# Low parts of some weight blocks made by an accumulating transfer instead of VectorE

## The chip, the cores and the metric

The kernel runs on one core of a Trainium2 chip. The engines that matter here are TensorE (PE in the profile; its weight loads are PEld), VectorE (DVE), ScalarE (ACT), GpSimd (POOL) and SyncE (SP), whose queue issues nearly all transfers. Each engine works through its own list of instructions in a fixed order and waits on semaphores for the others. The metric is device time in microseconds (us) of one launch. Before the change the median of three runs was 957.13 us, from 956.89 to 957.25.

## The reference

The reference is a trunk of two layers on 256 tokens of width 1024. Each layer adds half a SwiGLU feed-forward block, an attention mixer with an input and an output projection, and half a second SwiGLU block:

```python
def swiglu(h, w_gate, w_up, w_down):
    return (jax.nn.silu(h @ w_gate) * (h @ w_up)) @ w_down
for i in range(DEPTH):                       # DEPTH = 2, D_MODEL = 1024, D_FF = 2816
    h = rmsnorm(x, ffn1_norm[i])
    x = x + 0.5 * swiglu(h, ffn1_w_gate[i], ffn1_w_up[i], ffn1_w_down[i])
    ...                                      # mixer: w_in, attention, memory attention, w_out
    h = rmsnorm(x, ffn2_norm[i])
    x = x + 0.5 * swiglu(h, ffn2_w_gate[i], ffn2_w_up[i], ffn2_w_down[i])
```

All data is float32. The four feed-forward blocks hold most of the work.

## The kernel before, in words

**Three products for one.** TensorE multiplies in fp32r, a shorter float32. To keep float32 accuracy every operand is split: `hi` is the operand rounded to fp32r, and `lo` is what is left, `raw - hi`. A product is then three matmuls, hi by hi, lo by hi and hi by lo. They are lines 508, 511 and 514 in `dense`; the second one, line 511, is the first that reads `lo` of the weights. A matmul has 128 rows of weights by 512 columns.

**Weights come in chunks of 1 MB.** A chunk of a gate/up stage holds 4 row blocks of 128 rows, with 256 gate columns and 256 up columns each, so 128 partitions by 2048 elements. Group `g` (0 to 10) is 256 of the 2816 columns, and `c` (0 or 1) is the half of the 1024 rows. A plain gate/up chunk feeds 24 matmuls. `loader` gives each chunk one of three `raw` buffers and issues its two loads from SP (line 291). `split_hi` makes `hi` on ScalarE in two casts of 128x1024 (line 335), and `split_lo` makes `lo` on VectorE in two subtractions of 128x1024 (line 353). Four pairs of `hi` and `lo` buffers go round: the fifth chunk can't be cast before TensorE is done with the first. A `raw` buffer is free for another load when its chunk's `lo` is made.

**Stages.** A feed-forward block is a gate/up stage and a down stage. In the last three of the four blocks, groups 3 and 4 of the gate/up stage are made by seven block products instead of eight (`pair_items`, named m1 to m7, with sums of raw blocks, `wsum`, as operands). Their chunks and products lie between the plain chunks. The order there is, after groups 0 to 2: m1, (5,0), m5, (5,1), m7, (6,0), m6, (6,1), m3, (7,0), (7,1), m2, (8,0), m4, (8,1), (9,0), (9,1), (10,0), (10,1). A product `m` has 12 matmuls, and its result tile is `pair_m`; a plain chunk's result is `gu`.

**The planner.** The order of all instructions is written out at build time by `Flow`: each engine has a time when it is free, every step books a duration, and the generators `loader`, `split_hi` and `split_lo` go on when their conditions hold on that clock. On the chip only the order and the semaphores are left.

**Round trips.** The product of gate and up is transposed through DRAM: `hd<-hb` and `hr<-hd` (lines 640 and 646) are in the same SP queue as the weight loads. GpSimd has small work here: the powers of -1/2 of the norms (line 529).

## Time and profile before

| | |
|---|---|
| median of 3 runs | 957.13 us |
| profiled execution, its own time | 956.95 us |
| its span (first to last instruction) | 955.2 us |
| mean granted TensorE clock | 1.000 |
| gate/up stages that the change touches | about 318 to 435, 494 to 612, 776 to 894 us |

A profiled execution gives, for each engine, every instruction with its start and duration. The span is 1.75 us shorter than the execution's own time, which has the launch around it. Windows are given in us from the span's start. In the timeline a row has start, duration, engine, line, operation, output and inputs, and in square brackets idle time and what ended it. The share of busy time of TensorE is near to full everywhere, since its matmuls overlap (one is shown with 0.39 us, and starts 0.227 us after the one before it); the waits and the starts tell more than the share.

### The profile page before, as it was taken

The page shows a single profiled execution, that of the slowest core. Times are in us where ns is not written, and L with a number is a line of the kernel's source. Part 1 is how long each engine was busy: PE and PEld are TensorE (multiplying, and loading weights), DVE is VectorE, ACT ScalarE, POOL GpSimd, SP SyncE. Part 2 cuts the span into 40 slices and gives each one's busy share as a digit, 9 for nine tenths or more (in the row PEclk, how much of TensorE's full clock was granted, in tenths as well). Part 3 has the DMA queues.
Part 4 walks back from the last instruction along what each step waited for, and adds up shares of the span by engine and source line. Part 5 has one row for each costly group of instructions (what it writes and reads, how often), then busy time and mean ns, then how long its engine had stood idle before and what let it go on. Part 6 is the DMA issues. An engine that isn't in the chain of part 4 may idle for free.

```text
span 955.2 us, 13249 instructions
## 1 busy us (share of the span) xinstructions
PE 946.8 (99%) x4489; PEld 777.3 (81%) x4489; DVE 796.1 (83%) x1437; ACT 578.6 (61%) x1102; POOL 110.7 (12%) x160
## 2 busy tenths in 40 slices
PE   8999999999999999999999999999999999999998
PEld 7888888888877888888888888888887778888886
DVE  6767767688787899989889899896999888998884
ACT  6655555677676756647646656563676865665650
POOL 1000088322110100000000000000434200000000
PEclk9999999999999999999999999999999999999999
DMA  9988878486525376787746769775641367589751
GB/s 287 326 260 284 260 249 262 154 272 212 177 90 163 102 248 226 242 301 232 240 144 219 231 204 298 247 254 170 208 152 56 122 212 228 180 267 286 238 196 44
DMA packets 169294, 204.03 MB, mean 214 GB/s; under 512 B 9673, under 2 KB 144394, under 8 KB 169226
## 3 DMA queue, kind: packets, MB, share of 16 engines
q1 hardware_dynamic: 169226, 203.18, 66.3%
q8 instruction: 35, 0.57, 0.3%
q14 instruction: 33, 0.27, 0.1%
HBM read 188.99 MB, written 14.16 MB: 213 GB/s over the span
## 4 chain that ended last, share of the span: by engine, by line
PE 93%; DVE 4%; ACT 1%; DMA 1%; issue 0%; SPq 0%
PE gu L514 14%; PE gu L508 14%; PE gu L511 14%; PE acc L508 9%; PE acc L514 9%; PE acc L511 9%; PE pj L514 3%; PE pj L511 3%; PE pj L508 3%; PE pair_m L514 2%; PE pair_m L511 2%; PE pair_m L508 2%; DVE lo L353 1%; PE S L1335 1%; PE xtp L522 1%; PE AV L1416 1%
## 5 line engine op out<-in xcount | busy, mean ns | idle before, releaser
L335 ACT CAST hi<-raw 128x512 fp32r<-128x512 f32 (+1 forms) x469 | 339.1, 771 | 194.3 <-PE gu L514 75.5
L353 DVE TENSOR_TENSOR lo<-raw,hi 128x512 fp32r<-128x512 f32 (+1 forms) x469 | 394.6, 877 | 67.7 <-ACT hi L335 66.7
L514 PE MATMUL gu<-hi,xl 128*128 128x512 f32 x608 | 236.9, 390 | 0.4 <-DVE xl L559 0.4
L511 PE MATMUL gu<-lo,xh 128*128 128x512 f32 x608 | 236.8, 389 | 0.0
L508 PE MATMUL gu<-hi,xh 128*128 128x512 f32 x608 | 236.8, 389 | 0.0
L514 PEld LDWEIGHTS gu<-hi,xl 128*128 128x128 f32 x608 | 114.1, 188 | 24.5 <-DVE xl L559 0.8
L508 PEld LDWEIGHTS gu<-hi,xh 128*128 128x128 f32 x608 | 114.2, 188 | 23.5
L511 PEld LDWEIGHTS gu<-lo,xh 128*128 128x128 f32 x608 | 114.1, 188 | 23.5
L514 PE MATMUL acc<-hi,ht 128*128 128x512 f32 x280 | 109.5, 391 | 0.0
L508 PE MATMUL acc<-hi,ht 128*128 128x512 f32 x280 | 109.3, 390 | 0.0
L511 PE MATMUL acc<-lo,ht 128*128 128x512 f32 x280 | 109.1, 390 | 0.0
L511 PE MATMUL pj<-lo,xh 128*128 128x512 f32 x160 | 63.9, 400 | 0.0
L514 PE MATMUL pj<-hi,xl 128*128 128x512 f32 x160 | 63.8, 399 | 0.0
L508 PE MATMUL pj<-hi,xh 128*128 128x512 f32 x160 | 63.8, 399 | 0.0
L529 POOL TENSOR_TENSOR xr<-v,nhalf 128x1 f32<-128x1 f32 x12 | 11.7, 974 | 445.0 <-DVE v L527 445.0
L511 PEld LDWEIGHTS acc<-lo,ht 128*128 128x128 f32 x280 | 52.6, 188 | 10.9
L514 PEld LDWEIGHTS acc<-hi,ht 128*128 128x128 f32 x280 | 52.6, 188 | 10.8
L508 PEld LDWEIGHTS acc<-hi,ht 128*128 128x128 f32 x280 | 52.6, 188 | 10.7
L335 ACT CAST hi<-wsum 128x512 fp32r<-128x512 f32 x66 | 38.9, 620 | 20.5 <-DVE wsum L347 20.4
L623 ACT ACTIVATE sil<-gu,xr 128x256 f32<-128x256 f32 x76 | 35.7, 470 | 25.0 <-PE gu L514 24.9
L353 DVE TENSOR_TENSOR lo<-wsum,hi 128x512 fp32r<-128x512 f32 x66 | 42.5, 678 | 0.0
L529 POOL TENSOR_TENSOR hf<-v,nhalf 128x8 f32<-128x8 f32 (+1 forms) x20 | 31.7, 1584 | 90.1 <-DVE v L527 81.8
(231 smaller groups left out, 1356.6 us busy)
## 6 DMA issues: line engine op xcount, KB each, us to landing
raw<-in_ffn_w_down_dram SPq DMA_DIRECT2D x176, 256.0 KB, 4.3
raw<-in_ffn_w_gate_dram SPq DMA_DIRECT2D x86, 512.0 KB, 4.2
raw<-in_ffn_w_up_dram SPq DMA_DIRECT2D x86, 512.0 KB, 5.4
raw<-in_w_in_dram SPq DMA_DIRECT2D x32, 512.0 KB, 5.4
hd<-hb SPq DMA_DIRECT2D x44, 256.0 KB, 4.5
hr<-hd SPq DMA_DIRECT2D x44, 256.0 KB, 4.4
raw<-in_w_out_dram SPq DMA_DIRECT2D x8, 1024.0 KB, 4.8
raw<-in_w_mem_kv_dram SPq DMA_DIRECT2D x4, 1024.0 KB, 5.5
```

The source lines that it names most:

```text
L335: nc.scalar.copy(out=it.part(0, q, w), in_=src())
L353: nc.vector.tensor_sub(it.part(1, q, w), src(), it.part(0, q, w).bitcast(F32))
L508: nc.tensor.matmul(out=ps, lhsT=xh, rhs=wh, start=start, stop=False)
L511: nc.tensor.matmul(out=ps, lhsT=xh, rhs=wl, start=False, stop=False)
L514: nc.tensor.matmul(out=ps, lhsT=xl, rhs=wh, start=False, stop=stop)
L522: nc.tensor.transpose(out=dst, in_=src, identity=flip if flipped else ident)
L529: nc.gpsimd.tensor_tensor(out=dst, in0=v[:, :n], in1=nhalf[:, :n], op=ALU.pow)
L623: nc.scalar.activation(sil, ps[tb][:, 0:256], AF.Silu, scale=xt.r[tb])
L1335: nc.tensor.matmul(out=ss[e][:, pr, :nk], lhsT=q[rows, pr, :], rhs=k[rows, pr, :], start=i == 0, stop=i == len(passes) - 1)
L1416: nc.tensor.matmul(out=av[64 * e:64 * e + 64, pr, :], lhsT=vsrc(kb, pr, e), rhs=pts[e][:, pr, kb, :], start=(kb == 0), stop=(kb == nb - 1))
```

## The change

For four chunks in each of the last three gate/up stages, (6,1), (7,1), (8,1) and (9,1), VectorE's two subtractions are left out. ScalarE, after each cast to `hi`, writes minus that high part into the `lo` buffer: it rounds the raw block again with a factor of -1. Then GpSimd issues one transfer of 128x2048 that adds the raw block to what stands in `lo`. The planner books 7.0 us for it, and gives the `raw` buffer back after that. The lines after the new ones are moved down: line 335 is now 336, the new ScalarE step is line 339, the transfer is line 349, line 353 is now 371, lines 508 to 514 are 529 to 535, and the load of line 291 is 292.

```diff
@@ Item.__init__
             self.n, self.frees, self.takes, self.gives, self.guest = 1, 1, 0, 0, False
+            self.by_dma = False
@@ split_hi
                 nc.scalar.copy(out=it.part(0, q, w), in_=src())
                 t = flow.act(512 * w)
+                if it.by_dma:
+                    nc.scalar.activation(it.part(1, q, w), src(), AF.Copy, scale=-1.0)
+                    t = flow.act(512 * w)
                 it.hit[q:q + w] = [t] * w
+            if it.by_dma:
+                flow.spawn(lo_by_dma(it))
+
+    def lo_by_dma(it):
+
+        t = it.hit[3]
+        yield t
+        nc.gpsimd.dma_start(out=it.lo[0], in_=it.raws[0].raw, accum_op=ALU.add)
+        t = flow.now + 7.0
+        it.lot[0:4] = [t] * 4
+        yield t
+        raw_left[0] += it.frees
 
     def split_lo():
         for i, it in enumerate(items):
+            if it.by_dma:
+                continue
@@ plan
+    FOUR = ((6, 1), (7, 1), (8, 1), (9, 1))
+    BY_DMA = {(0, 1): (), (0, 2): FOUR, (1, 1): FOUR, (1, 2): FOUR}
@@ plan_ffn
                 gu[w] = add_chunk(parts(*w), 8, 2)
+                gu[w].by_dma = w in BY_DMA[l, nm]
```

The first place is ScalarE's list around chunk (6,1) of the first touched stage. Names carry the number of the chunk in the planner's list: 63 is the operand of m6, 64 is (6,1), 65 the operand of m3, 66 is (7,0) and 67 is (7,1). Before:

```order
L335 CAST hi63_0_3715<-wsum_3537 128x512
L335 CAST hi64_0_3778<-raw63_3701 128x1024 x2
L335 CAST hi65_0_3793<-raw61_3594 128x1024 x2
L335 CAST hi66_0_3827<-raw64_3728 128x1024 x2
L335 CAST hi67_0_3851<-raw65_3814 128x1024 x2
L623 ACTIVATE sil_3880<-gu0_3785,xr_2977 128x256
L655 CAST ht_3897<-hr_3841 128x512
```

And with the change:

```order
L336 CAST hi63_0_3715<-wsum_3537 128x512
L336 CAST hi64_0_3778<-raw63_3701 128x1024
L339 ACTIVATE lo64_0_3779<-raw63_3701 128x1024
L336 CAST hi64_0_3778<-raw63_3701 128x1024
L339 ACTIVATE lo64_0_3779<-raw63_3701 128x1024
L336 CAST hi65_0_3804<-raw61_3594 128x1024 x2
L336 CAST hi66_0_3824<-raw64_3728 128x1024 x2
L336 CAST hi67_0_3856<-raw65_3838 128x1024
L339 ACTIVATE lo67_0_3857<-raw65_3838 128x1024
L336 CAST hi67_0_3856<-raw65_3838 128x1024
L339 ACTIVATE lo67_0_3857<-raw65_3838 128x1024
```

Chunks 64 and 67 now take four steps of ScalarE each, with nothing else between them; the `sil` step has gone behind chunk 67.

The second place is SP's queue a little later, with what each row waits for: a DVE mark is VectorE's semaphore, a DMAHW mark one of the transfers that SP issues, and a DMASW mark one of the new transfers. `raw65` is loaded for chunk 67, `raw66` for the block of m2, `raw67` for (8,0) and `raw68` for (8,1). Before:

```order
L291 DMA raw65_3814<-in_ffn2_w_gate_dram 128x4x256 [waits DMAHW6_49,DMAHW5_49,DVE_49]
L291 DMA raw65_3814<-in_ffn2_w_up_dram 128x4x256
L291 DMA raw66_3834<-in_ffn2_w_gate_dram 128x4x256 [waits DVE_49]
L291 DMA raw66_3834<-in_ffn2_w_up_dram 128x4x256
L646 DMA hr_3841<-hd_3796 128x4x128 [waits DMAHW7_49,DMAHW2_49,Pool_49]
L291 DMA raw67_3856<-in_ffn2_w_gate_dram 128x4x256 [waits DMAHW1_49,DMAHW0_49,DVE_49]
L291 DMA raw67_3856<-in_ffn2_w_up_dram 128x4x256
L291 DMA raw68_3908<-in_ffn2_w_gate_dram 128x4x256 [waits DMAHW3_49,DMAHW4_49,DVE_49,Activation_49]
```

And with the change:

```order
L667 DMA hr_3834<-hd_3794 128x4x128 [waits DMAHW2_49,Pool_49]
L292 DMA raw65_3838<-in_ffn2_w_gate_dram 128x4x256 [waits DVE_49]
L292 DMA raw65_3838<-in_ffn2_w_up_dram 128x4x256 [waits DMAHW5_49]
L292 DMA raw66_3861<-in_ffn2_w_gate_dram 128x4x256 [waits DMAHW6_49,DMASW0_49]
L292 DMA raw66_3861<-in_ffn2_w_up_dram 128x4x256 [waits DMAHW7_49]
L292 DMA raw67_3864<-in_ffn2_w_gate_dram 128x4x256 [waits DMAHW1_49,DMAHW0_49,DVE_49]
L292 DMA raw67_3864<-in_ffn2_w_up_dram 128x4x256
L661 DMA hd_3949<-hb_3898 128x512 [waits DVE_49]
L292 DMA raw68_3956<-in_ffn2_w_gate_dram 128x4x256 [waits DMAHW4_49,DMAHW3_49,DMAHW5_49,DMASW1_49,Activation_49]
```

`raw65` now waits for VectorE's low part of chunk 65 instead of 64, `raw66` waits for the transfer of chunk 64, and `raw68` waits for the transfer of chunk 67.

The third place is GpSimd's list in the first two touched stages, where line 550 is the former line 529. With the change:

```order
L550 TENSOR_TENSOR xr<-v,nhalf 128x1 x2
L349 DMA lo_0_3779<-raw_3701 128x2048
L349 DMA lo_0_3857<-raw_3838 128x2048
L349 DMA lo_0_4026<-raw_3956 128x2048
L349 DMA lo_0_4105<-raw_4037 128x2048
L550 TENSOR_TENSOR xr<-v,nhalf 128x1 x2
L349 DMA lo_0_5389<-raw_5311 128x2048
L349 DMA lo_0_5467<-raw_5448 128x2048
L349 DMA lo_0_5636<-raw_5566 128x2048
L349 DMA lo_0_5715<-raw_5647 128x2048
L550 TENSOR_TENSOR xr<-v,nhalf 128x1
```

Before, the five `xr` steps stood there alone. The order of TensorE's instructions is the same before and after.

## The prediction

> **What bounds the kernel now.** I read first the engines' shares, then who TensorE waits for, then the three stages that the change touches. The page, the list of TensorE's waits over the whole span, and the busy time in the three gate/up stages and in a busy stretch of the first:

> ```profile
> PE 946.8 (99%) x4489; PEld 777.3 (81%) x4489; DVE 796.1 (83%) x1437; ACT 578.6 (61%) x1102; POOL 110.7 (12%) x160
> ...
> PE xtp L522 <- DMA x<-in_x_dram: 1.5, 2, 1.1
> PE warm L1621 <- POOL ident masks.py:199: 1.4, 1, 1.4
> PE otp L522 <- DVE of L1487: 0.5, 1, 0.5
> PE AV L1473 <- ACT PT L1349: 0.5, 1, 0.5
> PE gu L514 <- DVE xl L559: 0.4, 1, 0.4
> ...
> 318.00:435.00 117.00, 117.00 (x520) 96.92 (x519) 104.49 (x164) 69.95 (x109) 1.79 (x2) 1.00 0.72 233
> 494.00:612.00 118.00, 118.00 (x524) 97.77 (x523) 106.58 (x166) 70.43 (x108) 0.86 (x1) 1.00 0.75 241
> 776.00:894.00 118.00, 117.65 (x521) 97.11 (x520) 106.94 (x170) 72.39 (x113) 1.50 (x2) 1.00 0.74 234
> ...
> 400.00:410.00 10.00, 10.00 (x46) 8.26 (x44) 9.97 (x18) 5.91 (x8) 0.00 (x0) 1.00 1.02 323
> ```

> TensorE is the bound, and in the touched stages it is the whole bound: 520 matmuls in 117 us are 0.225 us each, the pace of its own stream, at a granted clock of 1.00. Of all its listed waits only 1.4 us lie behind 300 us, and none waits for a low part in these stages. VectorE is 89 to 91% busy there, ScalarE about 60%, the transfers 72 to 75% of the DMA engines, but all of that is done ahead of TensorE. So nothing that relieves VectorE can be seen at the end, and the question is only whether the new way of making `lo` is still done in time.

> How far ahead it is done is read at one chunk. The timeline around (6,1) of the first stage, ScalarE, VectorE and TensorE:

> ```profile
> 369.22 3.89 ACT L335 CAST hi<-raw 128x1024 fp32r<-128x1024 f32 x4
> 371.92 6.90 DVE L353 TENSOR_TENSOR lo<-raw,hi 128x1024 fp32r<-128x1024 f32 x6
> ...
> 378.04 0.39 PE L511 MATMUL gu<-lo,xh 128*128 128x512 f32 x1
> ```

> The first two casts of the row at 369.22 are this chunk's, the first two subtractions at 371.92 too (they end at about 374.3), and 378.04 is the first matmul on its `lo`, right after product m6. From the first cast to that matmul are 8.8 us, and the old way leaves 3.7 us over.

> **Part 1: VectorE loses, ScalarE gains.** The rows by form:

> ```profile
> L353 DVE TENSOR_TENSOR lo<-raw,hi 128x1024 fp32r<-128x1024 f32 x166 | 198.5, 1216 | 34.3 <-ACT hi L335 33.5 <-DMA grow<-in_mem_q_norm_dram 0.7
> L335 ACT CAST hi<-raw 128x1024 fp32r<-128x1024 f32 x166 | 168.8, 1049 | 106.0 <-PE gu L514 58.2 <-DMA raw<-in_ffn_w_up_dram 28.2 <-issue 10.6
> L571 ACT ACTIVATE junk<-x 128x512 bf16<-128x512 f32 x24 | 15.0, 624 | 0.0
> L335 ACT CAST hi<-raw 128x512 fp32r<-128x512 f32 x303 | 170.3, 619 | 88.3 <-PE acc L514 30.8 <-PE gu L514 17.4 <-issue 16.4
> ```

> 24 subtractions of 1.216 us, 29.2 us, leave VectorE. An ACTIVATE costs what a cast of the same width costs (624 and 619 ns), so 24 steps of 1.049 us, 25.2 us, come to ScalarE, 8.4 us a stage: from 60% to 67%. As work both count zero, since TensorE waits for neither; the cover is the lead of each chunk. But ScalarE's two extra steps lie in the chunk's own chain: four steps back to back took 3.89 us, with the hop to the next engine 4.0 us.

> **Part 2: the transfer.** 12 transfers of 1 MB that read two blocks and write one. No row shows an accumulating transfer, or one that GpSimd issues. The nearest rows are plain 1 MB transfers in one piece, issue to landing, and the spread of the loads between 360 and 410 us:

> ```profile
> raw<-in_w_out_dram SPq DMA_DIRECT2D x8, 1024.0 KB, 4.8
> raw<-in_w_mem_kv_dram SPq DMA_DIRECT2D x4, 1024.0 KB, 5.5
> ...
> DMA to landing us min/median/max: 4.1/5.2/9.6
> ```

> Call its time from issue to landing X. From below it is a plain transfer, 4.8. For the second read I add 1.05 MB at the 323 GB/s that the full engines moved (row at 400:410), 3.25 us: 8.1 to 8.8. From above it is the slowest landing, 9.6, plus a second read at the stage's mean of 234 GB/s, 4.5: 14.1. I take 8.5, by the 5.5 us row, since loads run beside it here. [...]

> Chunk (6,1): the low part is there at 369.22 + 4.0 + X = 373.2 + X, wanted at 378.04. It is late by X - 4.8: **3.7 us**. TensorE stands at this matmul, and all behind it moves by that.

> **Part 3: what is queued behind.** SP's queue and the timeline for (7,1) and (8,1):

> ```profile
> 374.30 0.37 SPq L291 DMA_DIRECT2D raw<-in_ffn_w_gate_dram  x1
> ...
> 379.97 1.05 ACT L335 CAST hi<-raw 128x1024 fp32r<-128x1024 f32 x1 [2.63 <-DMA raw<-in_ffn_w_up_dram]
> ...
> 385.52 0.37 SPq L291 DMA_DIRECT2D raw<-in_ffn_w_gate_dram  x1
> ...
> 391.64 0.39 PE L511 MATMUL gu<-lo,xh 128*128 128x512 f32 x1
> ...
> 396.62 0.39 PE L514 MATMUL gu<-hi,xl 128*128 128x512 f32 x1
> ...
> 398.58 0.47 ACT L623 ACTIVATE sil<-gu,xr 128x256 f32<-128x256 f32 x1
> 398.95 4.13 ACT L335 CAST hi<-raw 128x1024 fp32r<-128x1024 f32 x4
> ...
> 407.96 0.39 PE L511 MATMUL gu<-lo,xh 128*128 128x512 f32 x1
> ```

> (7,1): its load was issued at 374.30 and its cast began 5.67 us later. The load now waits for VectorE's part of the next chunk, which needs the casts after the four steps and ends at 373.2 + 1.0 + 2 x 1.2 = 376.6. Cast at 382.4, four steps, transfer: there at 386.4 + X. Wanted at 391.64 + (X - 4.8) = 386.8 + X. In time by 0.4, whatever X is: **0**.

> (8,1): its load waits for the transfer of (7,1), issue 386.4 + X, against 385.52 before. Cast at 392.1 + X; its buffers come free when (7,1) is done on TensorE, 397.0 + X - 4.8 = 392.2 + X, the same moment. Four steps and one `sil` of 0.5 between them, transfer: there at 396.7 + 2X, wanted at 407.96 + X - 4.8 = 403.2 + X. Late by X - 6.5: **2.0 us**.

> (9,1): its load doesn't wait for a transfer, and three chunks of TensorE time lie between its buffers' release and its use: 13.6 us, less 4.0 and 8.5. In time: **0**, as before.

> SP issues in order, so behind these waits also stand `raw66`, `raw67` and the round trips hd and hr; their results are wanted in the down stage, after 435, tens of us later: 0. On GpSimd nothing is queued behind the four issues until the next stage's `xr`.

> **The sum.** 5.7 us a stage. In the other two the distance from first cast to matmul is the same:

> ```profile
> 546.12 3.90 ACT L335 CAST hi<-raw 128x1024 fp32r<-128x1024 f32 x4
> 554.72 0.39 PE L511 MATMUL gu<-lo,xh 128*128 128x512 f32 x1
> ...
> 827.91 2.95 ACT L335 CAST hi<-raw 128x1024 fp32r<-128x1024 f32 x3
> 836.46 0.39 PE L511 MATMUL gu<-lo,xh 128*128 128x512 f32 x1
> ```

> 8.6 and 8.55 us against 8.82. Three stages are 17.1 us. On the profiled execution's 956.95 us that is 974.05; the median of the runs is 0.18 us above it, so I predict **974 us**. TensorE has no idle time behind the stages in which it could win this back. By X: 4.8 gives 957; 6.5 gives 962; 14.1 gives 9.3 + 7.6 = 16.9 a stage, 1008.

> **The rivals.**

> *Hidden.* X is near its lower bound, the transfers fit into the leads, and TensorE never waits. For it: the transfer needs no HBM, and the plain rows are at 4.8. Against it: two reads. Up to X = 5.4 it costs 3 x 0.6 = 1.8 us: 957 to 959. Chance 0.17. This is the case of no change, not slower.

> *Transfers far slower.* [...] At X = 20: 15.2 + 13.5 = 28.7 a stage, 86 us, 1043 us. No row speaks for or against it. Chance 0.13. [...]

> *Faster.* VectorE's relief shortens a wait of TensorE. There are 1.4 us of such waits after 300 us, and if all went it were 955.7 us, within 0.2%. Chance of more than that: 0.03.

> *ScalarE becomes the bound.* Its 67% is an average; if the `sil` steps that moved behind (7,1) held up the accumulators, each stage would lose about those 4 steps, 4.2 us, on top: 987 us. Against it: the accumulators of the next groups are others. Chance 0.05.

> **How the numbers follow.** The forecast, late at (6,1) and (8,1) with X from 5.4 to 14.1, has the remaining 0.62. The range takes in the hidden case and the upper bound of X: 957 to 1008. What this kernel's measurement can tell from no change is about 0.2%, 1.9 us. Faster 0.03, same 0.17, slower 0.80 (0.62 + 0.13 + 0.05).

> **What would show it.** In the profile of the changed kernel: the waits of TensorE get a row at the second matmul of a chunk (now line 532) that ends with the transfer, 12 or fewer times, with the longest near 3.7 us and a sum near 17. The transfers' time from issue to landing is X itself. ScalarE's new steps should take 1.05 us. The SP queue should wait about as long for the transfers as `raw68` is late. It is wrong if TensorE waits for none of this, if the transfers land within 5 us, or if (7,1) or (9,1) is a place of the largest wait.

## The result, and the profile after

The changed kernel takes 991.92 us, the median of 4 runs (990.29 to 994.95), beside 957.12 us for the kernel before on the same chip. The ratio is 1.036, with a 95% interval from 1.034 to 1.038: 34.8 us slower, where 17 were forecast. The profiled execution took 992.51 us, 35.6 more than the one of before.

The page of the changed kernel, TensorE's list of waits, and the two views of the new transfers. In the waits the columns are the sum, the number of times and the longest:

```profile
PE 959.3 (97%) x4489; PEld 784.5 (79%) x4489; DVE 770.6 (78%) x1413; ACT 601.9 (61%) x1126; POOL 120.9 (12%) x172
...
PE gu L532 <- DMA lo<-raw: 22.4, 6, 4.8
...
lo<-raw POOLq DMA_DIRECT2D x12, 1024.0 KB, 8.8
...
DMA to landing us min/median/max: 7.3/8.8/11.2
```

VectorE has 25.5 us less to do, and TensorE has a new wait, for the new transfers at the second matmul of a chunk. There are six, at (6,1) and (8,1) of each touched stage. They explain 22.4 of the 35.6 us. PE's busy time tells where more went: it grew by 12.5 us, for the same 4489 matmuls. The granted clock in the busy time by windows (columns: the window, its length, busy time and count of PE, PEld, DVE, ACT and POOL, then the granted clock, the DMA share and GB/s):

```profile
370.00:378.00 8.00, 8.00 (x36) 6.40 (x35) 5.55 (x8) 6.99 (x8) 1.10 (x1) 1.00 0.61 147
378.00:382.00 4.00, 0.25 (x2) 0.13 (x1) 3.75 (x5) 0.00 (x0) 0.00 (x0) 0.87 0.95 185
382.00:390.00 8.00, 8.00 (x24) 6.30 (x25) 0.66 (x2) 4.78 (x6) 0.87 (x1) 0.64 1.09 350
390.00:398.00 8.00, 8.00 (x37) 6.64 (x36) 7.55 (x13) 5.17 (x7) 0.00 (x0) 1.00 0.75 167
...
418.60:426.00 7.40, 7.40 (x26) 6.05 (x27) 2.53 (x4) 2.37 (x3) 0.00 (x0) 0.78 1.05 259
```

After the wait at 378 to 382, eight microseconds hold 24 matmuls where 36 or 37 stand before and after them, at a mean granted clock of 0.64. The last row is the stretch behind the wait of the first (8,1), with 0.78. The timeline of TensorE shows how long it lasts:

```profile
381.90 0.77 PE L532 MATMUL gu<-lo,xh 128*128 128x512 f32 x1 [3.75 <-DMA lo<-raw]
382.47 0.63 PE L535 MATMUL gu<-hi,xl 128*128 128x512 f32 x1
...
387.59 0.48 PE L535 MATMUL gu<-hi,xl 128*128 128x512 f32 x1
387.91 0.40 PE L529 MATMUL gu<-hi,xh 128*128 128x512 f32 x1
```

Matmuls start 0.43 us apart, half the pace, until about 387.7. Such a stretch comes with each of the six waits and stands at no other place of the three stages. The 24 matmuls after each wait take 2.9, 1.7, 1.7, 1.7, 2.1 and 1.6 us more than 24 times 0.227, together 11.7 us. With the waits this is 34.1 of the 35.6 us. Of the 1.5 us left, 1.0 belongs to the six waits too: the profile counts a wait from the end of the matmul before it, 0.39 us after its start, and the next one could have started after 0.227.

How the two late chunks come about is read from the other engines. GpSimd's issue for (6,1), SP's load for (7,1) and ScalarE's first cast of (7,1):

```profile
373.42 1.10 POOL L349 DMA_DIRECT2D lo<-raw  x1 [45.56 <-ACT lo L339]
...
376.46 0.37 SPq L292 DMA_DIRECT2D raw<-in_ffn_w_gate_dram  x1
...
384.90 1.04 ACT L336 CAST hi<-raw 128x1024 fp32r<-128x1024 f32 x1 [7.62 <-DMA raw<-in_ffn_w_up_dram]
```

The transfer of (6,1) is issued at 373.42 and has landed at 381.77, 8.35 us later; TensorE wanted it at 378.1. The load of `raw65` for (7,1) runs beside it and takes 8.4 us (376.46 to the cast at 384.90), where before the change it took 5.7. The kernel of the first experiment below has no such transfer, and the same load has landed there after 5.5 us. And around (8,1):

```profile
403.60 0.39 PE L529 MATMUL pair_m<-hi,xh 128*128 128x512 f32 x1
...
403.84 1.05 ACT L336 CAST hi<-raw 128x1024 fp32r<-128x1024 f32 x1 [1.26 <-PE gu L535]
...
408.40 0.86 POOL L349 DMA_DIRECT2D lo<-raw  x1 [18.42 <-ACT lo L339]
```

Here ScalarE waited for TensorE, not for a load: (8,1) takes over the `hi` and `lo` buffers of (7,1), and TensorE goes on from that chunk to m2 at 403.60. From there to the issue of the transfer are 4.8 us, the transfer takes 9.95, and TensorE has only 49 matmuls (m2, (8,0), m4 and one of (8,1) itself), 11.1 us, to do until it needs the result. 4.8 + 9.95 - 11.1 is 3.65 us late; the wait is 3.6.

### The profile page after: what moved, and what is told of

The parts are those of the page before. It is cut to its first block, busy times and chain, and to the rows that moved or that the text cites. A ratio compares the mean times of both kernels' runs of the same rounds, so it can differ in the third digit from the quotient of the medians.

```text
span 990.4 us, 13301 instructions
## 1 busy us (share of the span) xinstructions
PE 959.3 (97%) x4489; PEld 784.5 (79%) x4489; DVE 770.6 (78%) x1413; ACT 601.9 (61%) x1126; POOL 120.9 (12%) x172
## 4 chain that ended last, share of the span: by engine, by line
PE 86%; DMA 6%; DVE 4%; ACT 2%; issue 1%; SPq 0%; ACTq 0%; POOLq 0%
PE gu L532 13%; PE gu L535 13%; PE gu L529 13%; PE acc L529 8%; PE acc L535 8%; PE acc L532 8%; DMA lo<-raw 5%; PE pj L535 3%; PE pj L532 3%; PE pj L529 3%; DVE lo L371 1%; PE pair_m L532 1%; PE pair_m L535 1%; PE pair_m L529 1%; PE S L1356 1%
## 5 line engine op out<-in xcount | busy, mean ns | idle before, releaser
L371 DVE TENSOR_TENSOR lo<-raw,hi 128x512 fp32r<-128x512 f32 (+1 forms) x445 | 365.8, 859 | 99.5 <-ACT hi L336 99.3
L532 PE MATMUL gu<-lo,xh 128*128 128x512 f32 x608 | 242.5, 399 | 22.4 <-DMA lo<-raw 22.4
L535 PE MATMUL gu<-hi,xl 128*128 128x512 f32 x608 | 241.1, 397 | 0.4 <-DVE xl L580 0.4
L529 PE MATMUL gu<-hi,xh 128*128 128x512 f32 x608 | 240.6, 396 | 0.0
L532 PEld LDWEIGHTS gu<-lo,xh 128*128 128x128 f32 x608 | 116.9, 192 | 49.1 <-issue 13.8
L535 PEld LDWEIGHTS gu<-hi,xl 128*128 128x128 f32 x608 | 117.2, 193 | 25.1 <-DVE xl L580 0.8
L529 PEld LDWEIGHTS gu<-hi,xh 128*128 128x128 f32 x608 | 116.7, 192 | 24.9
L678 DVE TENSOR_TENSOR ht<-hr,ht 128x512 fp32r<-128x512 f32 x35 | 24.1, 688 | 34.6 <-ACT ht L676 34.6
## 6 DMA issues: line engine op xcount, KB each, us to landing
lo<-raw POOLq DMA_DIRECT2D x12, 1024.0 KB, 8.8
raw<-in_w_out_dram SPq DMA_DIRECT2D x8, 1024.0 KB, 4.8
```

Of the source, the lines that this page charges most:

```text
L371: nc.vector.tensor_sub(it.part(1, q, w), src(), it.part(0, q, w).bitcast(F32))
L529: nc.tensor.matmul(out=ps, lhsT=xh, rhs=wh, start=start, stop=False)
L532: nc.tensor.matmul(out=ps, lhsT=xh, rhs=wl, start=False, stop=False)
L535: nc.tensor.matmul(out=ps, lhsT=xl, rhs=wh, start=False, stop=stop)
L678: nc.vector.tensor_sub(lo, src, hi.bitcast(F32))
```

## The experiments

Two theories stand against each other. **Lateness**: the transfers end a chain that is longer than its lead, and TensorE pays for that, once as a wait and once as a lower clock that the wait brings. **Load**: the transfers or ScalarE's steps disturb the rest (clock, DMA engines, ScalarE), wherever they stand. Times of the kernel before beside the runs were 956.8 to 957.2 us.

### ScalarE's part alone

The transfer is replaced by two additions on VectorE; the steps of ScalarE stay.

```diff
-        nc.gpsimd.dma_start(out=it.lo[0], in_=it.raws[0].raw, accum_op=ALU.add)
-        t = flow.now + 7.0
-        it.lot[0:4] = [t] * 4
+        for q in (0, 2):
+            lo = it.part(1, q, 2)
+            nc.vector.tensor_add(lo, it.own(q, 2)(), lo.bitcast(F32))
+            t = flow.dve(1024)
+            it.lot[q:q + 2] = [t] * 2
```

> ScalarE's part of the change alone: it writes minus the high part into the low buffer as in the change, and the raw block is added to it by VectorE in two additions (in place of the transfer). Lateness theory (the loss is the waits of TensorE for transfers that land too late, 22.4 us in the profile of the change, and a halved TensorE clock for 3.4 or 6.8 us after each of the six long waits, some 12 us): VectorE's two additions end about 2 us later than the old subtractions, inside the leads of 3.5 us and more, so 957 us, within 1.5. Load theory (the added work itself costs, each step wherever it is): 25.2 us of ScalarE steps, 982 us at most.

Measured: 957.42 us, ratio 1.000 (0.999 to 1.001). VectorE's 24 additions in the groups by form:

```profile
L351 DVE TENSOR_TENSOR lo<-raw,lo 128x1024 fp32r<-128x1024 f32 x24 | 28.3, 1210 | 0.1
```

1.210 us each, they cost what the subtractions cost (1.216). So the 24 steps on ScalarE and the two more steps in the chunk's chain are free, and the whole loss comes with the transfer.

### The first chunk alone

```diff
-    FOUR = ((6, 1), (7, 1), (8, 1), (9, 1))
+    FOUR = ((6, 1),)
```

> The change for (6,1) alone: three transfers. Lateness theory: three waits of about 4 us, each followed by one or two windows of 3.4 us at half the clock (1.7 to 2.9 us more): 17 to 21 us, 974 to 978 us. Load theory: three transfers at 2.9 us: 966 us.

Measured: 976.54 us, ratio 1.020 (1.017 to 1.023). TensorE's waits, and two windows behind the first of them:

```profile
PE gu L532 <- DMA lo<-raw: 12.1, 3, 4.2
...
382.00:389.00 7.00, 6.96 (x24) 5.62 (x25) 2.90 (x4) 2.88 (x4) 0.00 (x0) 0.76 1.09 356
389.00:435.00 46.00, 46.00 (x205) 38.09 (x204) 40.94 (x69) 26.21 (x40) 0.00 (x0) 1.00 0.84 273
```

Three waits are 12.1 us, and three stretches of half clock add 1.7, 2.7 and 1.7 us, by the spacing of the matmuls. The sum, 18.2, is nearly all of what the profiled execution (975.80 us) lost, 18.85. One transfer a stage already costs more than was forecast for four.

### The last chunks of the stage

```diff
-    FOUR = ((6, 1), (7, 1), (8, 1), (9, 1))
+    FOUR = ((9, 1), (10, 1))
```

> The change for two chunks of each stage alone, (9,1) and (10,1), which have three chunks of TensorE time or more between the release of their buffers and their use, against two and a half or less for (6,1) and (8,1): six transfers instead of twelve. Lateness theory: none is late, TensorE waits for none, the clock stays at 1.00: 957 us, within 1.5. Load theory: six transfers at 34.8 / 12 = 2.9 us each: 974 us.

Measured: 960.41 us, ratio 1.004 (1.002 to 1.006): two microseconds above what was expected. TensorE waits twice for a transfer, 2.8 us in all:

```profile
PE gu L532 <- DMA lo<-raw: 2.8, 2, 1.7
...
DMA to landing us min/median/max: 8.2/9.1/11.1
```

Both are at (9,1), behind transfers of 10.5 and 11.1 us. In the changed kernel (9,1) was in time, with transfers as long (10.2 to 11.2 us), but behind waits that had held TensorE up. No lower clock follows these waits of 1.1 and 1.7 us. So six transfers cost 3.5 us where they are nearly in time, and twelve 34.8: it is the place that decides.

### Is the lower clock TensorE's idle time, or the transfers?

In the first kernel the wait is filled: 15 matmuls with a matrix of zeros as weights ahead of the one that waited at (6,1), 20 at (8,1). They add zero to the result. In this kernel and the next a pool of small buffers has 36 places instead of 48, which makes room for the zeros.

```diff
         flow.pe(T_MM)
         flow.step()
+        for _ in range(zero_jobs.pop(c.index, 0)):
+            nc.tensor.matmul(out=ps, lhsT=zero, rhs=wh, start=False, stop=False)
         nc.tensor.matmul(out=ps, lhsT=xh, rhs=wl, start=False, stop=False)
...
+    FILL = {(6, 1): 15, (8, 1): 20}
```

> The change, with extra matmuls by a block of zeros put ahead of the first matmul that reads the late low part, 15 at (6,1) and 20 at (8,1): 3.4 and 4.5 us of work that changes nothing in the sums and is done while TensorE would wait. The transfers are as late as before. If idle time lowers the clock: the clock stays at 1.00 and the 12 us of half clock go, 978 to 982 us, with waits of under 2 us left at these places. If the transfers themselves lower the clock, or if it is lowered by something else than idle time: half clock stays, 990 us or more.

The second is the kernel before, without any such transfer, in which TensorE waits at (6,1), (8,1) and (10,1) for 4 to 36 small steps of GpSimd.

```diff
+        if c.index in zero_jobs:
+            nc.tensor.matmul(out=ps, lhsT=zero, rhs=wh, start=False, stop=False)
+            for _ in range(zero_jobs.pop(c.index)):
+                nc.gpsimd.memset(zero.bitcast(F32), 0.0)
+            nc.tensor.matmul(out=ps, lhsT=zero, rhs=wh, start=False, stop=False)
```

> The kernel before, without any of the change, and TensorE made to stand at nine places: a matmul by zeros, then a row of memsets on GpSimd of the block of zeros that it read, then another matmul by zeros. At about 0.21 us a memset, 4 to 36 of them make idle times from about 1.2 to 8 us: in the first stage 4, 16 and 28, in the second 8, 20 and 32, in the third 12, 24 and 36, at (6,1), (8,1) and (10,1). If idle time alone lowers the clock, the longer ones are followed by 3.4 or 6.8 us at a granted clock of 0.5 and the shorter ones by none, with a limit somewhere between 0.7 us (no drop in the kernel before) and 3.3 us (drop in the changed kernel). If the transfers lower the clock: 1.00 everywhere. The sum of the idle times is 9 x 0.5 + 180 x 0.21 = 42 us, and 1.7 to 3.4 us for each drop: about 1010 us by the first, 999 by the second.

Measured: 987.64 us with the fill (ratio 1.032, 1.029 to 1.035), and the granted clock is whole again. TensorE's waits, the mean clock, and two windows of the first stage:

```profile
PE gu L540 <- DMA lo<-raw: 3.5, 6, 1.3
...
core 0: 984.7 us, clock 0.999
...
376.00:396.00 20.00, 19.30 (x84) 15.26 (x82) 11.99 (x17) 10.92 (x15) 0.87 (x1) 1.00 1.00 255
396.00:400.00 4.00, 2.85 (x13) 2.38 (x14) 4.00 (x8) 1.08 (x2) 0.00 (x0) 1.00 0.49 146
```

With the same transfers at the same places the clock stays at 1.00, so they don't lower it; idle time does. The time fell less than expected, for two reasons that the trace shows. The fill, 35 x 0.227 = 7.9 us a stage, was too long at (8,1) by 1.1, 1.7 and 0.9 us. And (7,1) is now late, by 1.4, 0.6 and 0.6 us: the wait at 397, in the second window. In the changed kernel the half clock covers that, since chunk (6,1) takes 8.0 us instead of 5.2. Taking off the 3.7 us of overlong fill leaves 983.1 of the profiled 986.85 us, so that lateness alone is worth some 26 us and the lower clock, net of what it hides, some 9.

The waits on GpSimd show the same from the other side. Two places of that kernel, an idle time of 1.12 and one of 2.22 us, and the window behind the second:

```profile
379.21 0.50 PE L520 MATMUL gu<-hi,zero 128*128 128x512 f32 x1 [1.12 <-POOL zero L519]
379.55 0.39 PE L521 MATMUL gu<-hi,xh 128*128 128x512 f32 x1
...
576.31 0.64 PE L520 MATMUL gu<-hi,zero 128*128 128x512 f32 x1 [2.22 <-POOL zero L519]
...
576.30:579.70 3.40, 3.39 (x8) 2.65 (x9) 1.37 (x3) 1.84 (x2) 0.00 (x0) 0.53 1.10 332
```

1.12 us cost nothing more; each of the eight idle times from 2.22 to 9.54 us brings matmuls at half pace, 1.7 to 3.0 us on top of the wait. The half clock lasts about 3.4, 6.8 or 10.2 us; behind the long ones a part of that lies in the idle time itself. No transfer of the change is in this kernel. One run took 1029.05 us, where about 1010 had been expected by this theory: the idle times add up to 48.4 us instead of 42, and the half clock cost 17.7 us more.

The length of a wait alone does not say whether half clock follows: a wait of 2.44 us further below has none, and one of 2.05 us has it. The traces hold the moments at which the granted clock changes, and in each kernel all of them lie on one grid of 3.413 us; in the changed kernel 380.95, 387.78, 418.50, 421.91 and 572.10 are 2, 9, 1 and 44 steps apart. In these two cases the idle time within one step of that grid tells the difference. Two steps around the wait of 2.44 us ((7,1) alone), and two around the one of 2.05 us (the plain copy):

```profile
390.49:393.90 3.41, 1.53 (x7) 0.94 (x5) 3.41 (x6) 1.61 (x3) 0.00 (x0) 1.00 0.80 195
393.90:397.31 3.41, 2.85 (x13) 2.40 (x14) 3.17 (x7) 0.63 (x2) 0.00 (x0) 1.00 0.44 123
```

```profile
585.36:588.77 3.41, 1.44 (x7) 0.86 (x5) 2.06 (x6) 3.41 (x5) 0.00 (x0) 1.00 0.87 302
588.77:592.18 3.41, 3.33 (x8) 2.68 (x9) 2.16 (x5) 1.51 (x5) 0.53 (x1) 0.50 1.05 313
```

The first wait is split into 1.88 and 0.56 us, and the clock stays at 1.00. Of the second 1.97 us lie in one step, and the next step is at 0.50.

### What the addition costs

The transfer becomes a plain copy of the raw block: the addition is left out, so the low part is not made.

```diff
-        nc.gpsimd.dma_start(out=it.lo[0], in_=it.raws[0].raw, accum_op=ALU.add)
+        nc.gpsimd.dma_start(out=it.lo[0], in_=it.raws[0].raw)
```

> The change with a plain copy in place of the adding transfer: raw to low part, same size, same queue, same order. It leaves out the addition, so the low parts are wrong and only the time counts. If the second read of the addition is the cost (8.8 us median, against 4.8 to 5.5 us for plain 1 MB transfers): 5 to 6 us from issue to landing, waits of TensorE under 1 us a place, 957 to 963 us. If it is GpSimd's issue and the load of the DMA engines: 8 to 9 us still, and about 990 us.

Measured: 966.83 us in one run, a little more than expected. Issue to landing:

```profile
DMA to landing us min/median/max: 4.2/6.2/10.2
```

At (6,1) the copies took 4.46, 4.20 and 4.32 us, the adding transfers 8.35, 8.20 and 8.22. So the adding transfer takes 4 us longer at this place. Not all of that is the addition, since the longer transfer has more of the load of `raw65` beside it (0.5 MB against 0.3): in the last experiment below, two adding transfers with no load beside them took 7.1 and 7.7 us, so the addition itself is nearer 3 us. Without it (6,1) is in time in two stages and 0.9 us late in the third. What remains of the loss are 6.3 us of waits, most of them at (8,1), where the copy takes 7.0 us, and one stretch of half clock behind the longest, 2.05 us.

### Two smaller transfers

Each half block is sent off as soon as ScalarE has made its part.

```diff
+                if it.by_dma:
+                    flow.spawn(lo_by_dma(it, q))
...
-        nc.gpsimd.dma_start(out=it.lo[0], in_=it.raws[0].raw, accum_op=ALU.add)
+        nc.gpsimd.dma_start(out=it.part(1, q, 2), in_=it.own(q, 2)(), accum_op=ALU.add)
```

> The change with each transfer cut in two of 128x1024, the first issued as soon as the first half's minus high part is written, 2 us earlier than the whole. The matmuls use the first half for the first 6 of 24 matmuls, 1.4 us. Lateness theory, with a half transfer at 6 to 7 us: the first half late by at most 1 us, the second by 1 to 2 us at (6,1), less at (8,1); waits of 1 to 2 us in place of 4, too short for a drop of the clock: 957 + 6 x 1.5 = 962 to 968 us. If the cost is by the transfer, or twice as many issues cost more: 992 us or more.

Measured: 987.11 us, ratio 1.032 (1.029 to 1.034), far from what was expected. Waits and transfers:

```profile
PE gu L533 <- DMA lo<-raw: 17.6, 14, 2.9
...
DMA to landing us min/median/max: 5.1/7.3/10.4
```

A half takes 5.1 to 5.3 us at its best, at (6,1), and the whole 8.2: halving the size saves 3 us, not 4. From the two follow, as an estimate (the loads beside them are not the same), about 2 us that don't depend on the size and 6 us for each MB. Two halves hold the chain longer than one whole, and (7,1), (8,1) and (9,1) are now late as well, 14 waits, and only the longest, of 2.9 us, brought half clock. The kernel is 4.8 us faster than the changed one, where 24 to 30 had been expected. In the profiled execution the listed waits are 4.8 us less and the half clock is 1.8 us instead of 11.7, but 2.2 us are lost behind the touched stages and 1.9 at the start, and each of the many waits costs some 0.16 us (0.39 - 0.227) more than its listed length. Why the places behind the stages got slower was not tried.

### Minus the high part first

ScalarE writes minus the high part from the raw block alone, so both such steps can go ahead of the casts, and the transfer is sent two steps earlier.

```diff
+            if it.by_dma:
+                for src, q, w, dep in it.units:
+                    yield calm_a(i)
+                    nc.scalar.activation(it.part(1, q, w), src(), AF.Copy, scale=-1.0)
+                    t = flow.act(512 * w)
+                flow.spawn(lo_by_dma(it, t))
             for src, q, w, dep in it.units:
...
-                if it.by_dma:
-                    nc.scalar.activation(it.part(1, q, w), src(), AF.Copy, scale=-1.0)
-                    t = flow.act(512 * w)
```

> The change with ScalarE's steps in another order: both steps that write minus the high part come first, then the transfer is issued, then the two casts follow while it is under way. Each transfer starts 2 us earlier. Theory (the loss is the latency of a chain of raw load, ScalarE, transfer, and the next raw load that waits for it, plus half clock after waits of over 2 us): at (6,1) late by 1.8 us in place of 3.8, at (7,1) 1 to 2 and at (8,1) 1 to 2, all too short for a drop of the clock: 4 to 5 us a stage, 969 to 973 us, granted clock 1.00 in the three stages. If the lateness were set by something else than the start of the transfer (the load of the DMA engines), the waits would stay as they are: 985 us or more.

Measured: 986.25 us, ratio 1.030 (1.029 to 1.031), far above what was expected. At (6,1) it does what it should: late by 1.8, 2.0 and 1.5 us instead of 3.8, 3.8 and 4.8, with no stretch of half clock there. But the next chunk is late instead (TensorE's waits and timeline, SP and ScalarE):

```profile
PE gu L532 <- DMA lo<-raw: 15.0, 6, 3.7
...
381.46 0.50 PE L532 MATMUL gu<-lo,xh 128*128 128x512 f32 x1 [1.77 <-DMA lo<-raw]
399.02 0.80 PE L532 MATMUL gu<-lo,xh 128*128 128x512 f32 x1 [3.66 <-DMA lo<-raw]
...
381.48 0.37 SPq L292 DMA_DIRECT2D raw<-in_ffn_w_gate_dram  x1
...
387.17 2.01 ACT L332 ACTIVATE lo<-raw 128x1024 fp32r<-128x1024 f32 x2 [8.11 <-DMA raw<-in_ffn_w_up_dram]
```

The load for (7,1) is issued at 381.48, when the transfer of (6,1) has landed, and not at 376.46 as in the changed kernel: in this build the load has to wait for that transfer, 6.5 us in SP's list, since `raw65` gets the buffer that the transfer reads. So the lateness was handed on through the `raw` buffer, with half clock at (7,1) in all three stages, 6.2 us. The waits for transfers are 15.0 us; 2.4 us more are waits for `h`, behind the touched stages.

### (7,1) back on VectorE, and (7,1) alone

What makes (8,1) late: the buffers of (7,1) that TensorE frees, or the transfer of (7,1)? And has (7,1) a lead of its own?

```diff
-    FOUR = ((6, 1), (7, 1), (8, 1), (9, 1))
+    FOUR = ((6, 1), (8, 1), (9, 1))      # first kernel
+    FOUR = ((7, 1),)                     # second kernel
```

> Chunks (6,1), (8,1) and (9,1) by transfer, (7,1) by VectorE again. It asks what makes (8,1) late. Theory (the buffer loop): ScalarE may cast (8,1) only when TensorE is done with (7,1), whose hi and lo buffers it takes over; from there run four ScalarE steps with a sil between them (4.3 us), 0.5 of hops and the transfer (9.3 to 10), against 11.1 us of TensorE work (49 matmuls of 0.227). None of this depends on how (7,1) itself was made: the waits at (8,1) stay at 3 to 4 us in each stage, (6,1) stays at 3.7 to 5, and the time is that of the change, 989 to 993. Rival (the prediction's step): the load of (8,1) waits for the transfer of (7,1), and this makes it late; without that transfer (8,1) is in time, three waits of 3.5 us and their clock drops of about 1.6 us are gone, 975 to 978.

> Only chunk (7,1) by transfer, nothing ahead of it in the stage. Theory: in the change (7,1) is in time only because the waits and the half clock at (6,1) push TensorE back. Alone, its cast starts as before the change at about 380.0 in the first stage, its transfer is issued 4.1 us later and lands after 8.3 to 9.0 us at 392.4 to 393.1, wanted at 391.64: a wait of 0.8 to 1.5 us in each stage, too short for a drop of the clock, 959 to 962. Rival (the chunk has lead enough by itself): no wait, 956.5 to 957.5.

Measured: 983.73 us without (7,1), ratio 1.028 (1.026 to 1.030), between the two expectations; 961.40 us with (7,1) alone, ratio 1.004 (1.003 to 1.006), as expected. Without (7,1), TensorE's waits, SP's load for (8,1), ScalarE's cast of it, and the window of its transfer; in a second fence the load and the window of the transfer in the changed kernel:

```profile
PE gu L532 <- DMA lo<-raw: 16.7, 6, 4.0
...
388.63 0.37 SPq L292 DMA_DIRECT2D raw<-in_ffn_w_gate_dram  x1
...
403.90 1.05 ACT L336 CAST hi<-raw 128x1024 fp32r<-128x1024 f32 x1 [1.26 <-issue]
...
408.40:416.50 8.10, 6.53 (x29) 5.07 (x27) 5.63 (x11) 7.06 (x11) 1.15 (x2) 1.00 0.92 189
```

```profile
397.33 0.37 SPq L292 DMA_DIRECT2D raw<-in_ffn_w_gate_dram  x1
...
408.40:418.40 10.00, 6.46 (x29) 5.03 (x27) 7.14 (x15) 7.95 (x12) 1.72 (x2) 1.00 1.01 263
```

The cast of (8,1) starts at 403.90 against 403.84, its transfer at 408.48 against 408.40: the start does not depend on the transfer of (7,1), it is set by TensorE's release of the buffers. But the transfer takes 8.04 us instead of 9.95, and TensorE waits 1.7 us instead of 3.6, in the other stages 1.8 and 1.7 instead of 3.5 and 2.9, and no half clock follows. Its load, `raw68`, is issued at 388.63 instead of 397.33 (there it has landed at 402.55, still ahead of the cast). The next two loads are issued at about the same times in both kernels, but with `raw68` among them they land later, the gate part of the last at 410.78 instead of 406.94, and more is loaded beside the transfer: 263 GB/s in all against 189. Less the 1.05 MB of the transfer itself, that is 1.6 MB beside it against 0.5. So the transfer of (7,1) does make (8,1) later, not through its start but by pushing loads towards the time of its transfer. Both theories had half of it.

With (7,1) alone the waits are 2.4, 1.1 and 1.0 us:

```profile
PE gu L532 <- DMA lo<-raw: 4.5, 3, 2.4
...
394.46 0.47 PE L532 MATMUL gu<-lo,xh 128*128 128x512 f32 x1 [2.44 <-DMA lo<-raw]
```

So (7,1) has no lead of its own either. In the changed kernel it was in time because TensorE had been held up at (6,1).

### The same transfer where VectorE is nearly full

In the mixer of layer 1, at about 680 to 760 us, VectorE is busy for 94 and 97% of the two windows below, and TensorE does stand now and then, in the two longest of these waits 0.5 us for VectorE and 0.5 for ScalarE. There no gate/up chunk is made by transfer, but the last two chunks of `w_in` are, in the form with minus the high part first; and in another kernel the last four.

```diff
-    FOUR = ((6, 1), (7, 1), (8, 1), (9, 1))
+    FOUR = ()
...
+        if l == 1:
+            for it in [c for b in plan[l, "in"] for c in b][8:] + plan[l, "out"][0:0]:    # [6:] in the other kernel
+                it.by_dma = True
```

> The same way of making low parts (minus high parts first, then the adding transfer), put where VectorE sets the pace: the last two chunks of the input projection of layer 1, which have leads of 13 us before, and none of the gate/up chunks. VectorE loses 8 subtractions of 0.69 us, 5.5 us, in a stretch in which it is 97% busy, ScalarE gets 8 steps of 0.62 us. Where a relieved VectorE helps: TensorE's small waits between 680 and 780 us shrink, 952 to 956 us. If the transfers, issued from GpSimd between the small steps of the norms that stand on the chain there, hold those up: 957 to 962 us.

> As the run with two chunks of the input projection, but the last four, whose leads are 10 to 13 us before: 11 us of VectorE's work taken away. If VectorE's relief is worth time: 950 to 955 us, better than with two. If the transfers of 8 to 10 us come too late for the two chunks with leads of 10 to 12 us, or hold up GpSimd's small steps: slower than with two, 957 to 965 us.

Measured: two chunks 954.67 us, ratio 0.9975 (0.9966 to 0.9985), the only version that beats the kernel before, if by little; four chunks 958.41 us, ratio 1.002 (1.000 to 1.003). The stretch in the kernel before, and then with two chunks, there with the window of the first transfer ahead:

```profile
720.00:730.00 10.00, 9.34 (x53) 6.90 (x52) 9.35 (x21) 6.38 (x22) 4.18 (x5) 1.00 0.01 3
730.00:740.00 10.00, 9.91 (x59) 7.79 (x57) 9.69 (x26) 8.67 (x31) 3.48 (x4) 1.00 0.11 20
```

```profile
710.90:718.03 7.13, 7.13 (x36) 5.88 (x36) 5.56 (x10) 6.36 (x16) 6.04 (x7) 1.00 0.73 147
...
720.00:730.00 10.00, 10.00 (x59) 8.23 (x58) 9.38 (x23) 7.44 (x24) 4.76 (x5) 1.00 0.85 208
730.00:740.00 10.00, 10.00 (x60) 8.23 (x59) 9.69 (x27) 8.82 (x32) 4.26 (x4) 1.00 0.24 99
```

TensorE is busy all the time now, 0.75 us more of these 20, and no transfer is late (7.1 and 9.0 us). The first runs alone: 147 GB/s for 7.13 us are its own 1.05 MB. Matmul by matmul, TensorE gains 2.5 us on the kernel before between 690 and 785 us, as much as the medians differ; the profiled execution gave it back at the start, where TensorE stands 3.0 us for a late load of `x` (1.5 before). How much of the 2.5 us is VectorE's relief is not shown, since the planner wrote another order for TensorE in this stretch too. With four chunks two transfers are late, and the gain is gone; the longer wait, 1.7 us, is behind a transfer of 7.8 us, the other behind one of 11.2:

```profile
PE pj L535 <- DMA lo<-raw: 1.9, 2, 1.7
```

## Why the prediction was right or wrong

**What bounds the kernel**: right. VectorE's busy time fell by 25.5 us and ScalarE's new steps took 25.3, and with VectorE's additions in place of the transfer the time did not move (957.42 us).

**The transfer's time X, 8.5 us**: right as a median (8.8) and at (6,1) (8.2 to 8.35), and its make-up roughly so: 5.5 for the transfer and 3.25 for the second read were booked, the plain copy took 4.2 to 4.5, and the addition some 3, with the load beside it on top. It is not one number, though: from 7.3 to 11.2 by what is loaded beside it.

**(6,1) late by 3.7 us**: right, 3.75, 3.8 and 4.8 us; in the third stage the first cast began 7.6 us ahead of that matmul's turn instead of the 8.55 booked.

**(7,1): 0, whatever X is**: the wait was 0, but the reason given held only for a TensorE held up at (6,1). The load of `raw65` took 8.4 us beside the transfer, where 5.67 had been carried over from before; with the transfer, 8.16 us, that makes the low part 1.9 us late even against the pushed-back TensorE. The half clock hid it, as the fill (1.4, 0.6, 0.6 us late) shows.

**(8,1): 2.0 us**: too small, 3.6, 3.5 and 2.9. The step had both chains, the load behind the transfer of (7,1) and the buffers that TensorE frees, meeting at the same moment; it was the second alone. The size missed because X was taken as 8.5 at a place where it is 9.3 to 9.95, with 1.4 to 1.6 MB loaded beside it, and 0.3 of hops. Where it was 8.04, the lateness was 1.7, near the forecast.

**(9,1): 0**: measured 0, but again behind the earlier waits; with (9,1) and (10,1) alone it was late twice. Of the 13.6 us 9.6 are left for the transfer, and the two late ones took 10.5 and 11.1, where 8.5 was booked.

**The sum: the step that failed** is "TensorE stands at this matmul, and all behind it moves by that". A wait was booked at its own length. What the runs showed in its place: a wait that put 1.89 us or more of idle time into one step of the clock's grid, behind 300 us, was followed by half clock for 3.4 to 10.2 us, in which TensorE lost 1.6 to 3.0 us more. Three waits at (6,1) alone cost 12.1 us and their half clock 6.1. In the changed kernel this missing term is 11.7 us gross, about 9 net of what it hides; the other 5.3 us of waits (22.4 for 17.1) are mostly (8,1), and the last 1.5 us lie mostly in what the listed length of a wait leaves out.

**The rivals.** Hidden: no, X is never below 7.3. Transfers far slower than 14 us: no, the longest took 11.2, and no run shows the 20 us that its sum was made with. ScalarE the bound: no, by the run without the transfer. Faster through VectorE's relief: not here, as TensorE has nothing to win back in these stages; in the mixer of layer 1 the kernel got 0.25% faster for two chunks.

## What to carry to other kernels

A wait on TensorE is not worth its length alone: in these runs, behind 300 us, one under 1.9 us never brought half clock, all from 2.6 us on did, and in between it hung on how the wait fell on the grid. A forecast of a long wait needs that second term, 1.6 to 3.0 us each here. A transfer that takes work from an engine is costed by the chunk's lead (when its buffers are free, when its result is wanted), place by place and with what is loaded beside it, since a chunk that is in time behind a late one may have no lead of its own. The one place where such a transfer paid, by 2.5 us, was a stretch in which the relieved engine is nearly full, and there for two chunks that landed in time and not for four.
